# Row softmax on one core: two 30-row loads in place of four 15-row loads, and one 30-row store in place of two

## The chip, the cores and the metric

The kernel runs on one core of a Trainium2 chip. The metric is device time in microseconds (us) of one execution. Before the change it is 159.98 us, the median of three executions (159.98, 159.98 and 159.81).

## What is computed

The input is a float32 array of 16 x 1024 x 512. Each of its 16,384 rows of 512 numbers is divided by 2 and put through a softmax:

```python
x_scaled = x / 2.0
x_max = np.max(x_scaled, axis=-1, keepdims=True)
exp_x = np.exp(x_scaled - x_max)
return exp_x / np.sum(exp_x, axis=-1, keepdims=True)
```

33.55 MB are read and 33.55 MB are written.

## The kernel before

**Rows and tiles.** A row is 2,048 bytes. The 16,384 rows are spread over 128 partitions, 128 rows to each. `TILES` (lines 10 to 12) cuts these 128 into ten tiles of 3, 5 and eight times 15 rows per partition. A tile takes a block of consecutive rows of the input, and inside it each partition has `r` consecutive rows: a 15-row tile is, for each partition, one run of 30,720 bytes, both in DRAM and in the on-chip buffer. That buffer, `arena`, holds 98 rows per partition. Tiles 0 to 7 fill it. Tiles 8 and 9 go to its first 30 rows, where tiles 0, 1, 2 and a part of 3 were, so they can be loaded only when these have been stored (`LATE`, line 14).

**Compute.** ScalarE takes the exponential of x/2 in place, one row at a time, and adds the row up on the way (line 206 for the first three rows, line 275 for the others, in a loop over groups of five rows that waits at line 142 until the tile of the group has landed). VectorE takes the reciprocal of the sums (line 168) and multiplies the rows by it in place (line 171), one 15-row tile at a time, the last tile in three pieces of five rows. The maximum is not subtracted; at the end lines 182 to 198 count the rows whose sum lies in a safe interval, and if any row's does not, the whole is computed again in the plain way (lines 220 to 259). That does not happen with this input.

**Transfers and their order.** Three engines issue DMAs, each on a queue of its own:

- SyncE (SP) loads tile 0 and issues all stores in the order of the tiles (lines 213 to 216). Each store waits until the multiply of its tile is done (line 135).
- ScalarE loads tile 1 ahead of everything (line 157) and then issues the loads of tiles 2 to 7 one behind the other (lines 159 to 161), ahead of its table load and its first exponential.
- GpSimd (POOL) loads tiles 8 and 9 (lines 178 to 181). For tile 8 it waits until the exponentials of tile 6 are done (row 83, `TURN`) and until tiles 0, 1 and 2 are stored; for tile 9 until tile 3 is stored.

**The slow store.** The store of tile 1 (`SPREAD`) is cut in three by `pieces` (lines 116 to 120): four rows of all 128 partitions (8,192 bytes each), then the fifth row (2,048 bytes) of 126 partitions, then that of the last two partitions. Ahead of the store of tile 2, SP waits until all these pieces have landed:

```python
for t in range(len(tiles)):
    if t == SPREAD + 1:
        nc.sync.wait_ge(s_home[min(LATE)], landings(range(t)))
    store(nc.sync, t)
```

So the stores of tile 2 and of all later tiles are held until the last two small rows are in DRAM.

Of the kernel before, what the change touches and what calls it, by code (L numbers as in the profile page):

```python
# [10 lines left out]
    (3, 0), (5, 3), (15, 8), (15, 23), (15, 38), (15, 53), (15, 68), (15, 83), (15, 0), (15, 15),  # L11
]

LATE = {8: (0, 1, 2), 9: (3,)}
ARENA = 98

HEAD = [3]
# [2 lines left out]
SPREAD = 1  # L20
# [8 lines left out]
def kernel(  # L29
# [5 lines left out]
    nc = tc.nc  # L35
# [6 lines left out]
    xf = x.flatten_outer_dims()  # L42
    of = out.flatten_outer_dims()
    N, D = xf.shape
    P = nc.NUM_PARTITIONS
# [14 lines left out]
    tiles, base = [], 0  # L60
# [2 lines left out]
        tiles.append((base, r, at))  # L63
        base += r

    def dram(ap, t):
        b, r, _ = tiles[t]
        return ap[b * P : (b + r) * P].rearrange("(p r) d -> p r d", r=r)

    def sb(t):  # L70
        _, r, at = tiles[t]
        return arena[:, at : at + r, :]

    straight = sum(HEAD)
# [3 lines left out]
    owner = [max(t for t, (b, _, _) in enumerate(tiles) if b <= s) for s in starts]  # L78
# [9 lines left out]
            pairs.append([k])  # L88
    upto = [1 + max(j for j, ks in enumerate(pairs) if owner[ks[0]] == t) for t in range(len(tiles))]

    ld = [nc.alloc_semaphore(f"ld{t}") for t in range(len(tiles))]
    s_home = {t: nc.alloc_semaphore(f"s_home{t}") for t in LATE}
    s_near = nc.alloc_semaphore("s_near")
    s_end = nc.alloc_semaphore("s_end")
    s_exp = nc.alloc_semaphore("s_exp")
    s_go = nc.alloc_semaphore("s_go")
    s_rec = nc.alloc_semaphore("s_rec")
    s_mul = nc.alloc_semaphore("s_mul")
# [11 lines left out]
    g_rec = nc.alloc_semaphore("g_rec")  # L110
    g_mul = nc.alloc_semaphore("g_mul")

    def load(eng, t):
        eng.dma_start(out=sb(t), in_=dram(xf, t)).then_inc(ld[t], 16)  # L114

    def pieces(t):
        r = tiles[t][1]
        if t == SPREAD:
            return [(0, P, 0, r - 1), (0, 126, r - 1, r), (126, P, r - 1, r)]
        return [(0, P, 0, r)]  # L120

    stored_by = {u: s_home[t] for t, us in LATE.items() for u in us}
    for t, (_, r, at) in enumerate(tiles):
        over = {u for u, (_, ru, au) in enumerate(tiles[:t]) if at < au + ru and au < at + r}
        assert over <= {u for v, us in LATE.items() if v <= t for u in us}

    def landings(ts):
        return 16 * sum(len(pieces(t)) for t in ts)

    near = len(tiles) - 2  # L130
    sem_of = {**stored_by, near: s_near}
    at_end = landings(t for t in range(len(tiles)) if t not in sem_of)

    def store(eng, t):
        eng.wait_ge(s_mul, upto[t])
        for p, q, lo, hi in pieces(t):
            eng.dma_start(
                out=dram(of, t)[p:q, lo:hi], in_=sb(t)[p:q, lo:hi]
            ).then_inc(sem_of.get(t, s_end), 16)

    def take(eng, sem, n):
        eng.wait_ge(sem, n).then_inc(sem, -n)  # L142

    def rounds(eng, body):


        i = eng.alloc_register("general")
        eng.wait_ge(s_near, 16)
        eng.wait_ge(s_flag, 1)
        eng.reg_load(i, flag[0:1, 0:1])  # L150
        with eng.While(lambda: eng.snap(i, min_val=0, max_val=1) < 1):
            body()
            eng.reg_add(i, i, 1)

    def early():
        load(nc.sync, 0)
        load(nc.scalar, 1)

    def loads():
        for t in range(2, min(LATE)):  # L160
            load(nc.scalar, t)

    def program():

        for j, ks in enumerate(pairs):
            b, c = starts[ks[0]], sum(sizes[k] for k in ks)
            a = b % ARENA
            nc.vector.reciprocal(  # L168
                out=recip[:, b : b + c], in_=stats[:, b : b + c]
            )._wait_ge(s_exp, ks[-1] + 1).then_inc(s_rec, 1)  # L170
            nc.vector.tensor_mul(  # L171
                out=arena[:, a : a + c],
                in0=arena[:, a : a + c],
                in1=recip[:, b : b + c].unsqueeze(2).to_broadcast([P, c, D]),
            )._wait_ge(s_rec, j + 1).then_inc(s_mul, 1)

        nc.gpsimd.memset(ones[:, :], 1.0).then_inc(s_ones, 1)  # L177
        nc.gpsimd.wait_ge(s_exp, starts.index(TURN))
        for t, us in LATE.items():
            nc.gpsimd.wait_ge(s_home[t], landings(us))  # L180
            load(nc.gpsimd, t)
        nc.gpsimd.tensor_scalar(  # L182
            out=inside[:, :], in0=stats[:, :], scalar1=LO, scalar2=HI,
            op0=Alu.max, op1=Alu.min,
        )._wait_ge(s_exp, len(sizes)).then_inc(s_cnt, 1)
        nc.vector.scalar_tensor_tensor(  # L186
            out=inside[:, :], in0=inside[:, :], scalar=1.0, in1=stats[:, :],
            op0=Alu.mult, op1=Alu.is_equal, accum_out=count[:, :],
        )._wait_ge(s_cnt, 1).then_inc(s_cnt, 1)
        nc.vector.tensor_scalar(  # L190
            out=flag[:, :], in0=total[:, :], scalar1=float(N), scalar2=None, op0=Alu.is_ge,
        )._wait_ge(s_tot, 1).then_inc(s_flag, 1)


        for t in range(len(tiles)):
            nc.tensor.wait_ge(ld[t], 16).then_inc(s_go, owner.count(t))
        nc.tensor.wait_ge(s_ones, 1)
        nc.tensor.matmul(  # L198
            total[:, :], lhsT=count[:, :], rhs=ones[:, :], start=True, stop=True
        )._wait_ge(s_cnt, 2).then_inc(s_tot, 1)  # L200

        nc.scalar.preload_act_table(Exp)  # L202
        for k, c in enumerate(HEAD):
            take(nc.scalar, s_go, 1)
            for b in range(starts[k], starts[k] + c):
                ins = nc.scalar.activation(  # L206
                    out=arena[:, b], in_=arena[:, b], func=Exp, scale=0.5,
                    accum_out=stats[:, b : b + 1],
                )
            ins.then_inc(s_exp, 1)  # L210
        exponentials(straight, n_rows)

        for t in range(len(tiles)):
            if t == SPREAD + 1:
                nc.sync.wait_ge(s_home[min(LATE)], landings(range(t)))
            store(nc.sync, t)

        x_g = xf.rearrange("(t p r) d -> t p r d", p=P, r=G)  # L220
        o_g = of.rearrange("(t p r) d -> t p r d", p=P, r=G)
        data = arena[:, 0:G]

        def vector():
            for i in range(n_rows // G):
                nc.vector.reduce_max(
                    out=g_max[:, :], in_=data, axis=mybir.AxisListType.X, negate=True
                )._wait_ge(g_go, i + 1).then_inc(g_top, 1)
                nc.vector.reduce_sum(
                    out=g_sum[:, :], in_=data, axis=mybir.AxisListType.X  # L230
                )._wait_ge(g_exp, i + 1).then_inc(g_add, 1)
                nc.vector.reciprocal(
                    out=g_sum[:, :], in_=g_sum[:, :]
                )._wait_ge(g_add, i + 1).then_inc(g_rec, 1)

        def scalar():
            for i in range(n_rows // G):
                nc.scalar.activation(out=data, in_=data, func=Exp, scale=0.5)._wait_ge(
                    g_sub, i + 1
                ).then_inc(g_exp, 1)  # L240

        def gpsimd():
            nc.gpsimd.wait_ge(s_end, at_end)
            for i in range(n_rows // G):
                nc.gpsimd.dma_start(out=data, in_=x_g[i]).then_inc(g_ld, 16)
                nc.gpsimd.wait_ge(g_ld, 16 * (i + 1)).then_inc(g_go, 1)
                nc.gpsimd.tensor_add(
                    out=data, in0=data, in1=g_max[:, :].unsqueeze(2).to_broadcast([P, G, D])
                )._wait_ge(g_top, i + 1).then_inc(g_sub, 1)
                nc.gpsimd.tensor_mul(  # L250
                    out=data, in0=data, in1=g_sum[:, :].unsqueeze(2).to_broadcast([P, G, D])
                )._wait_ge(g_rec, i + 1).then_inc(g_mul, 1)
                nc.gpsimd.wait_ge(g_mul, i + 1)
                nc.gpsimd.dma_start(out=o_g[i], in_=data).then_inc(g_st, 16)
                nc.gpsimd.wait_ge(g_st, 16 * (i + 1))

        rounds(nc.vector, vector)
        rounds(nc.scalar, scalar)
        rounds(nc.gpsimd, gpsimd)
        nc.sync.wait_ge(s_near, 16)  # L260
        nc.sync.wait_ge(s_end, at_end)
# [26 lines left out]
    first = list(entry.instructions)  # L288
    at = next(k for k, i in enumerate(head) if type(i).__name__ == "InstDrain")
    entry.instructions = head[:at] + first + head[at:]  # L290
    act = []
    entry.instructions = list(entry.instructions) + [i for i in jumps if i not in act]
    nc.switch_body(here, parent=None, valid_engines=[i.engine for i in jumps])
    loads()
    program()


# [28 lines left out]
```

## Time and profile before

| what | value |
|---|---|
| median of three executions | 159.98 us |
| the profiled execution, its own time | 159.75 us |
| its span, first to last instruction | 158.4 us |
| bytes moved by DMA | 67.11 MB |
| busy ScalarE | 80.6 us (51%) |
| busy VectorE | 73.2 us (46%) |
| exponentials of a 15-row tile | 15 rows, about 0.61 us apart |
| multiply of a 15-row tile | 8.16 us |
| last multiply ends | 128.8 us |

The page has the busy shares of the engines in 40 slices of the span, and below them the busy share of the core's 16 DMA engines and what they moved. In the DMA part, q10 is ScalarE's queue, q1 is SP's and q0 is GpSimd's; a packet is what one DMA engine moves in one go, and the packets of four bytes tell a semaphore that an engine has finished its part of a transfer. A view of a stretch of time counts the packets that begin in it. The list of waits says, for each engine, what it waited for, how long in total, how many times, and the longest; SPq is SP's own sequencer, which issues stores.

### The profile page before, as it was taken

What the parts mean: (1) busy time and instruction counts of PE and PEld (TensorE: products, weight loads), DVE (VectorE), ACT (ScalarE), POOL (GpSimd) and SP (SyncE); (2) the same over time, 40 slices, a digit from 0 to 9 for tenths busy, and PEclk for the clock granted to TensorE, in tenths of its full rate; (3) what the DMA queues carried; (4) which work ended last, traced back from release to release, by engine and by line L of the source; (5) the groups of instructions that cost most, each with busy time, mean ns of one, the idle gap of its engine ahead of it and who ended that gap; (6) DMA issues with size and microseconds to landing.
All of it is one profiled execution on the core that took longest, in us unless ns stands there. A gap on an engine that the chain in (4) does not pass through costs nothing. (4 is left out here: it accounts for less than half of the span.)

```text
span 158.4 us, 658 instructions
## 1 busy us (share of the span) xinstructions
PE 0.2 (0%) x2; PEld 0.1 (0%) x2; DVE 73.2 (46%) x27; ACT 80.6 (51%) x257; POOL 2.2 (1%) x8
## 2 busy tenths in 40 slices
PE   0000000000000000000000000000000000000000
PEld 0000000000000000000000000000000000000000
DVE  0066000992994979903970029808927960000000
ACT  0780399598899980795005971991059700000000
POOL 0000000000000000001000010000000100000000
DMA  7999998999999999999898989898989898989896
GB/s 270 469 411 383 461 439 357 446 470 412 395 502 389 442 427 427 442 411 458 388 481 380 489 380 489 380 489 380 489 372 496 372 489 380 489 380 489 380 481 264
DMA packets 3024, 67.11 MB, mean 424 GB/s; under 512 B 336, under 2 KB 336, under 8 KB 720
## 3 DMA queue, kind: packets, MB, share of 16 engines
q1 hardware_dynamic: 1728, 34.34, 50.7%
q10 hardware_dynamic: 1008, 24.90, 37.0%
q0 software_dynamic: 288, 7.86, 11.5%
HBM read 33.55 MB, written 33.55 MB: 424 GB/s over the span
## 5 line engine op out<-in xcount | busy, mean ns | idle before, releaser
L275 ACT ACTIVATE arena<-arena x125 | 76.7, 615 | 40.2 <-ACTq L142 40.2
L171 DVE TENSOR_TENSOR arena<-arena,recip 128x7680 f32<-128x7680 f32 (+2 forms) x12 | 70.2, 5847 | 0.4
L168 DVE RECIPROCAL recip<-stats 128x15 f32<-128x15 f32 (+2 forms) x12 | 2.7, 224 | 55.5 <-ACT arena L275 47.3
L275 ACT ACTIVATION_READ_ACCUMULATOR arena<-arena x125 | 23.4, 187 | 0.0
L202 ACT ACT_TABLE_LOAD x1 | 1.3, 1283 | 5.0 <-issue 5.0
L114 POOL DMA_DIRECT2D arena<-in_x_dram x2 | 1.3, 631 | 90.3 <-ACT arena L275 72.3
L206 ACT ACTIVATE arena<-arena 128x512 f32<-128x512 f32 x3 | 1.9, 618 | 0.0
L182 POOL TENSOR_SCALAR inside<-stats 128x128 f32<-128x128 f32 x1 | 0.6, 631 | 32.6 <-ACT arena L275 32.6
L206 ACT ACTIVATION_READ_ACCUMULATOR arena<-arena 128x1 f32 x3 | 0.6, 185 | 0.0
L198 PE MATMUL total<-ones,count 128*1 128x1 f32 x2 | 0.2, 164 | 129.1 <-DVE inside L186 129.1
L186 DVE SCALAR_TENSOR_TENSOR inside<-inside,stats 128x128 f32<-128x128 f32 x1 | 0.3, 284 | 0.0
L190 DVE TENSOR_SCALAR flag<-total 1x1 int32<-1x1 f32 x1 | 0.1, 147 | 0.3 <-PE total L198 0.3
L198 PEld LDWEIGHTS total<-ones,count 128*1 128x1 f32 x2 | 0.1, 80 | 129.1 <-DVE inside L186 129.1
L177 POOL MEMSET ones<- 128x1 f32 x1 | 0.1, 99 | 1.1 <-POOLq L37 1.1
L310 POOL MEMSET const-float32-0.0<- 128x1 f32 x1 | 0.1, 105 | 0.2 <-issue 0.2
L310 POOL MEMSET const-bfloat16-1.0<- 128x1 bf16 x1 | 0.1, 108 | 0.0
L310 POOL MEMSET const-uint8-127<- 128x1 uint8 x1 | 0.1, 108 | 0.0
L310 POOL MEMSET const-float32-1.0<- 128x1 f32 x1 | 0.1, 105 | 0.0
L186 DVE DVE_READ_ACCUMULATOR inside<-inside,stats 128x1 f32 x1 | 0.1, 83 | 0.0
## 6 DMA issues: line engine op xcount, KB each, us to landing
out_dram<-arena SPq DMA_DIRECT2D x8, 3840.0 KB, 42.9
arena<-in_x_dram ACTq DMA_DIRECT2D x6, 3840.0 KB, 41.7
arena<-in_x_dram POOLq DMA_DIRECT2D x2, 3840.0 KB, 23.7
arena<-in_x_dram ACTq DMA_DIRECT2D x1, 1280.0 KB, 7.3
out_dram<-arena SPq DMA_DIRECT2D x1, 1024.0 KB
arena<-in_x_dram SPq DMA_DIRECT2D x1, 768.0 KB, 5.9
out_dram<-arena SPq DMA_DIRECT2D x1, 768.0 KB
out_dram<-arena SPq DMA_DIRECT2D x1, 252.0 KB
```

What stands on the lines that cost most here:

```text
L114: eng.dma_start(out=sb(t), in_=dram(xf, t)).then_inc(ld[t], 16)
L168: nc.vector.reciprocal(out=recip[:, b : b + c], in_=stats[:, b : b + c])._wait_ge(s_exp, ks[-1] + 1).then_inc(s_rec, 1)
L171: nc.vector.tensor_mul(out=arena[:, a : a + c], in0=arena[:, a : a + c], in1=recip[:, b : b + c].unsqueeze(2).to_broadcast([P, c, D]),)._w ...
L177: nc.gpsimd.memset(ones[:, :], 1.0).then_inc(s_ones, 1)
L182: nc.gpsimd.tensor_scalar(out=inside[:, :], in0=stats[:, :], scalar1=LO, scalar2=HI, op0=Alu.max, op1=Alu.min,)._wait_ge(s_exp, len(sizes) ...
L186: nc.vector.scalar_tensor_tensor(out=inside[:, :], in0=inside[:, :], scalar=1.0, in1=stats[:, :], op0=Alu.mult, op1=Alu.is_equal, accum_ou ...
L190: nc.vector.tensor_scalar(out=flag[:, :], in0=total[:, :], scalar1=float(N), scalar2=None, op0=Alu.is_ge,)._wait_ge(s_tot, 1).then_inc(s_f ...
L198: nc.tensor.matmul(total[:, :], lhsT=count[:, :], rhs=ones[:, :], start=True, stop=True)._wait_ge(s_cnt, 2).then_inc(s_tot, 1)
L202: nc.scalar.preload_act_table(Exp)
L206: ins = nc.scalar.activation(out=arena[:, b], in_=arena[:, b], func=Exp, scale=0.5, accum_out=stats[:, b : b + 1],)
L275: ins = nc.scalar.activation(out=data, in_=data, func=Exp, scale=0.5, accum_out=stats[:, r : n_rows - E + 1 + r][:, bass.ds(now, 1)],)
L310: nc = _bacc.Bacc("TRN2", target_bir_lowering=False, num_devices=1)
```

## The change

Loads and stores get lists of their own. The tiles, the arena, the exponentials and the multiplies stay as they are; what changes is which tiles share one DMA.

- Tiles 4 and 5 are loaded by one DMA, and so are tiles 6 and 7. Such a pair is one block of rows: each partition has 30 consecutive rows, a run of 61,440 bytes.
- Tiles 6 and 7 are also stored by one DMA of 30 rows, which waits for the multiplies of both. Tiles 4 and 5 are stored one at a time: each store writes half of a partition's run of 30 rows.
- Row groups of a pair may begin when the whole pair has landed, since a pair has one semaphore.
- `LATE` and the semaphores are counted by load, so tile 8 is load 6 and tile 9 load 7; what they wait for is the same.

On the queues: ScalarE issues five loads where it issued seven (10,240 bytes per partition, two of 30,720, two of 61,440), SP eleven store DMAs where it issued twelve, GpSimd two as before. The order of instructions on VectorE, GpSimd and TensorE is the same.

```diff
-LATE = {8: (0, 1, 2), 9: (3,)}
+LOADS = [(0,), (1,), (2,), (3,), (4, 5), (6, 7), (8,), (9,)]
+STORES = [(0,), (1,), (2,), (3,), (4,), (5,), (6, 7), (8,), (9,)]
+
+LATE = {6: (0, 1, 2), 7: (3,)}
...
-    def dram(ap, t):
-        b, r, _ = tiles[t]
-        return ap[b * P : (b + r) * P].rearrange("(p r) d -> p r d", r=r)
...
+    def dram(ap, ts):
+        b, r, _ = span(ts)
+        first, rows, _ = next(blocks[k] for k, us in enumerate(LOADS) if ts[0] in us)
+        assert first <= b and b + r <= first + rows
+        block = ap[first * P : (first + rows) * P].rearrange("(p r) d -> p r d", r=rows)
+        return block[:, b - first : b - first + r]
...
-    def load(eng, t):
-        eng.dma_start(out=sb(t), in_=dram(xf, t)).then_inc(ld[t], 16)
+    def load(eng, k):
+        eng.dma_start(out=sb(LOADS[k]), in_=dram(xf, LOADS[k])).then_inc(ld[k], 16)
...
-    def store(eng, t):
-        eng.wait_ge(s_mul, upto[t])
-        for p, q, lo, hi in pieces(t):
+    def store(eng, j):
+        ts = STORES[j]
+        eng.wait_ge(s_mul, upto[ts[-1]])
+        for p, q, lo, hi in pieces(j):
             eng.dma_start(
-                out=dram(of, t)[p:q, lo:hi], in_=sb(t)[p:q, lo:hi]
-            ).then_inc(sem_of.get(t, s_end), 16)
+                out=dram(of, ts)[p:q, lo:hi], in_=sb(ts)[p:q, lo:hi]
+            ).then_inc(sem_of.get(j, s_end), 16)
...
-        for t in range(len(tiles)):
-            nc.tensor.wait_ge(ld[t], 16).then_inc(s_go, owner.count(t))
+        for k, ts in enumerate(LOADS):
+            nc.tensor.wait_ge(ld[k], 16).then_inc(
+                s_go, sum(owner.count(t) for t in ts)
+            )
...
-        for t in range(len(tiles)):
-            if t == SPREAD + 1:
-                nc.sync.wait_ge(s_home[min(LATE)], landings(range(t)))
-            store(nc.sync, t)
+        for j in range(len(STORES)):
+            if j == SPREAD + 1:
+                nc.sync.wait_ge(s_home[min(LATE)], landings(range(j)))
+            store(nc.sync, j)
```

`span(ts)` gives the first row, the number of rows and the place in the arena of a group of tiles that lie behind one another.

More of the change, by code (lines that the diff above doesn't have):

```diff
@@ L64, with span, sb @@
         base += r
-    def dram(ap, t):
-        b, r, _ = tiles[t]
-        return ap[b * P : (b + r) * P].rearrange("(p r) d -> p r d", r=r)
-    def sb(t):
-        _, r, at = tiles[t]
+    def span(ts):
+        assert all(tiles[u][2] == tiles[t][2] + tiles[t][1] for t, u in zip(ts, ts[1:]))
+        return tiles[ts[0]][0], sum(tiles[t][1] for t in ts), tiles[ts[0]][2]
+    for part in (LOADS, STORES):
+        assert [t for ts in part for t in ts] == list(range(len(tiles)))
+    blocks = [span(ts) for ts in LOADS]
+    def dram(ap, ts):
[4 more added lines that the diff above has]
+        return block[:, b - first : b - first + r]
+    def sb(ts):
+        _, r, at = span(ts)
         return arena[:, at : at + r, :]
@@ L89 @@
     upto = [1 + max(j for j, ks in enumerate(pairs) if owner[ks[0]] == t) for t in range(len(tiles))]
-    ld = [nc.alloc_semaphore(f"ld{t}") for t in range(len(tiles))]
-    s_home = {t: nc.alloc_semaphore(f"s_home{t}") for t in LATE}
+    ld = [nc.alloc_semaphore(f"ld{k}") for k in range(len(blocks))]
+    s_home = {k: nc.alloc_semaphore(f"s_home{k}") for k in LATE}
     s_near = nc.alloc_semaphore("s_near")
@@ L111, with pieces, landings @@
     g_mul = nc.alloc_semaphore("g_mul")
-    def load(eng, t):
-        eng.dma_start(out=sb(t), in_=dram(xf, t)).then_inc(ld[t], 16)
-    def pieces(t):
-        r = tiles[t][1]
-        if t == SPREAD:
+    def load(eng, k):
+        eng.dma_start(out=sb(LOADS[k]), in_=dram(xf, LOADS[k])).then_inc(ld[k], 16)
+    def pieces(j):
+        r = span(STORES[j])[1]
+        if STORES[j] == (SPREAD,):
             return [(0, P, 0, r - 1), (0, 126, r - 1, r), (126, P, r - 1, r)]
         return [(0, P, 0, r)]
[L122 to L130, printed above, removed]
-    sem_of = {**stored_by, near: s_near}
-    at_end = landings(t for t in range(len(tiles)) if t not in sem_of)
-    def store(eng, t):
-        eng.wait_ge(s_mul, upto[t])
-        for p, q, lo, hi in pieces(t):
+    stored_by = {j: s_home[k] for k, js in LATE.items() for j in js}
+    for k, (_, r, at) in enumerate(blocks):
+        over = {
+            j for j, ts in enumerate(STORES)
+            if ts[0] < LOADS[k][0] and span(ts)[2] < at + r and at < span(ts)[2] + span(ts)[1]
+        }
+        assert over <= {j for v, js in LATE.items() if v <= k for j in js}
+    def landings(js):
+        return 16 * sum(len(pieces(j)) for j in js)
+    near = len(STORES) - 2
+    sem_of = {**stored_by, near: s_near}
+    at_end = landings(j for j in range(len(STORES)) if j not in sem_of)
+    def store(eng, j):
+        ts = STORES[j]
+        eng.wait_ge(s_mul, upto[ts[-1]])
+        for p, q, lo, hi in pieces(j):
             eng.dma_start(
-                out=dram(of, t)[p:q, lo:hi], in_=sb(t)[p:q, lo:hi]
-            ).then_inc(sem_of.get(t, s_end), 16)
+                out=dram(of, ts)[p:q, lo:hi], in_=sb(ts)[p:q, lo:hi]
+            ).then_inc(sem_of.get(j, s_end), 16)
     def take(eng, sem, n):
@@ L159, in loads @@
     def loads():
-        for t in range(2, min(LATE)):
-            load(nc.scalar, t)
+        for k in range(2, min(LATE)):
+            load(nc.scalar, k)
     def program():
@@ L178, in program @@
         nc.gpsimd.wait_ge(s_exp, starts.index(TURN))
-        for t, us in LATE.items():
-            nc.gpsimd.wait_ge(s_home[t], landings(us))
-            load(nc.gpsimd, t)
+        for k, js in LATE.items():
+            nc.gpsimd.wait_ge(s_home[k], landings(js))
+            load(nc.gpsimd, k)
         nc.gpsimd.tensor_scalar(
```

## The prediction

> **What bounds the kernel now.** I read the page's slices first, then the DMA part by stretches of time, then SP's list of waits and its instructions in order of time.
>
> ```profile
> DMA  7999998999999999999898989898989898989896
> GB/s 270 469 411 383 461 439 357 446 470 412 395 502 389 442 427 427 442 411 458 388 481 380 489 380 489 380 489 380 489 372 496 372 489 380 489 380 489 380 481 264
> HBM read 33.55 MB, written 33.55 MB: 424 GB/s over the span
> SPq L261 <- DMA out_dram<-arena: 29.2, 1, 29.2
> ```
>
> The DMA engines are busy in every slice, while ScalarE and VectorE are busy for about half of the span. SP's last wait, 29.2 us, is for stores alone: when the last multiply ends (128.8), three tiles' stores are still to move. The chain of waits ends there too, so compute sets nothing. By the packet records a full packet of 30,720 bytes takes 1.138 us on its engine, and 16 such streams give 432 GB/s; 67.11 MB at that rate are 155.3 us. The span holds 3 us more: the start, the end and small dips. What a change can do is to leave the DMA engines idle somewhere (each idle us is then a us at the end), or to shave these 3 us.
>
> ```profile
> q10 hardware_dynamic: 162, 4.49, 94.5%
> q1 hardware_dynamic: 141, 0.26, 6.1%
> ```
>
> This is the stretch from 37 to 48 us. Loads (q10) and the small rows of the slow store (q1) begin nearly as many packets, 162 and 141, though the ones hold seventeen times the bytes of the others. An engine gives the two queues a turn each, and a turn is one packet, whatever its size. In the packet records the semaphore packet of four bytes takes a turn as well.
>
> ```profile
> SPq L137 <- DMA out_dram<-arena: 13.0, 1, 13.0
> 49.08 0.36 SPq L137 DMA_DIRECT2D out_dram<-arena  x1
> q10 hardware_dynamic: 60, 1.66, 89.1%
> ```
>
> The first two lines, of SP's waits and of its instructions, show the hold: SP waits 13 us for tile 1's rows and issues tile 2's store at 49.08. The last small rows begin at 48.42 and 48.43 and their semaphore packets at 48.50 and 48.52, just as the load of tile 5 ends (its semaphore packets: 48.32 to 48.79). The third line is the stretch from 48.55 to 53: q1 begins no packet, and q10, with tiles 6 and 7 still to load, covers the 4 us until tile 2's store moves at 53. **This cover is what the change takes away.**
>
> **The loads, part by part.** A pair is one run of 61,440 bytes per partition, so I take one packet per partition. By the rows, packets of 2,048, 8,192 and 30,720 bytes take 0.084, 0.309 and 1.138 us: 0.0368 us per 1,000 bytes and 0.008 us each. One of 61,440 then takes 2.268 us, and a pair gives each engine 8 data packets and one semaphore packet, as one tile did. Until 27.9 us, when tile 3's load runs out, nothing changes but the start (below). From 27.9 on the records of before show the small rows taking their turns against 18 turns of loads, those of tiles 4 and 5, and ending with them. Now the 18 turns are those of both pairs. So the last small row ends with the last pair:
>
> - loads after 27.9: 16 packets x 2.268 = 36.3 us on each engine
> - small rows between them: 11.3% of the stretch from 28 to 48.55 us went to q1, 2.3 us
> - end of pair and small rows: 27.9 + 36.3 + 2.3 = 66.5 us
>
> At that moment all of tiles 0 to 7 is loaded; GpSimd's load of tile 8 cannot be issued until tile 2 is stored; and all later stores stand behind SP's wait, tiles 2 and 3 with their multiplies long done (36 and 47 us). All three queues are empty. The idle time:
>
> - from the semaphore packet to SP's issue: 49.08 - 48.52 = 0.56 us
> - from the issue to the first packet: the view does not show it for a store on idle engines. Nearest is the first load of the kernel, issued at 0.00 on idle engines:
>
> ```profile
> DMA  0000000000000000999480036779999497979994
> ```
>
> The stretch is 0 to 2.5 us in 40 slices; the first 16 are empty, 1.0 us, and by the packet records 14 of the 16 engines have begun at 1.29. I take 1.15. The other row is SP's issues under load, 10.22 and 49.08, whose packets came 3.9 us later or more; there load packets stood ahead, so it is the upper bound.
> - first packets begin slowly: the kernel's first 16 took 0.50 us in the mean where later ones took 0.234. I take 0.25, between 0 and 0.5.
>
> Together 0.56 + 1.15 + 0.25 = **1.96 us**, at the low end 1.56, with the loaded row 4.7.
>
> The Trainium skill ("DMA: Bandwidth & Descriptors", section "Latency and other measured facts") puts the first byte of such a DMA at about 0.6 us; in place of 1.15 that would be an estimate of 1.41 us of idle time. The trace's 1.0 speaks against it, though for a load.
>
> **What it saves.** 24 packets fewer per engine (16 of loads, 8 of the paired store) x 0.008 = 0.19 us. In the packet records the stretch from 52 to 54 us, where tile 2's store breaks in, moves 407 GB/s in place of 432: 0.12 us, which goes. The three DMAs fewer save no boundary: the records show tile 4's load beginning where tile 3's ended. ScalarE issues two loads fewer ahead of its table load (7 take 4.80 us), so the first exponential, at 6.25, waits for tile 0 (landed 5.90) and comes 0.2 to 0.3 us earlier, and so does the first store. At the end this gives nothing, since the DMA engines are busy anyway; it may move the small rows by one turn (first rival).
>
> **What comes later and is covered.** The first pair lands at about 48.5; tile 4 landed at 39.8 before. Exponentials of tile 4 move from 40.2 to about 49, those of tiles 5, 6 and 7 follow at 58, 68 and 77 (9.2 us a tile), multiplies 8.4 us behind each. Stores of tiles 2 and 3 run from 68 to 90, so stores 4 and 5 (multiplied by 67 and 76) are in time, and so is the store of 6 and 7 (95 us; its turn comes at about 123). Writing halves of 30-row runs changes no packet size; I cost it at nothing, and the one-sided risk of a slower DRAM pattern stays in the range. GpSimd waits for tile 2's store to land (about 79) where exponentials ended last before (73.9). Tile 8 moves from about 83 to 101 and tile 9 to 120, one turn each against stores. Its multiplies end by 133, against 128.8 before, and the last store's turn is at 150. So 17 us of cover stay, and nothing of this is on the path.
>
> **Sum.** 159.75 + 1.96 - 0.19 - 0.12 = **161.4 us**, made against the profiled execution's own 159.75 (span 158.4), which is 0.23 below the median shown.
>
> **The rivals.**
>
> 1. *The small rows finish a turn or two ahead of the last load packet* (not slower). Then SP issues at about 65, under the cover of a packet of 2.27 us, and the engines never run dry: 159.75 - 0.31 = 159.4 to 159.8. For it: the earlier start of 0.2 to 0.3 us is a quarter of a turn of 1.138, and turns at times come in twos. Against it: in before the last row came after tile 5's last packet on both engines that carry it, and both must be early. Chance 0.18.
> 2. *The run of 61,440 bytes is moved as two packets or more* (the change does not do what it says). Turns stay as they were, the hold ends at 49, and tiles 6 and 7 load beside stores 2 and 3 until 82 but land together at 84. Tile 8's load is then issued at 94 in place of 73.9, tile 9's last multiply is done at about 142, and the last store's turn is at 149: still covered, 159.7. For it: no packet in this trace is larger than 30,720. Against it: 30,720 itself is not cut, nor is any smaller run. Chance 0.10.
> 3. *A turn is several packets.* Then the small rows would be done early, with no idle time: 159.5. The records show singles, doubles at times. The Trainium skill ("DMA: Bandwidth & Descriptors", "Queues, rings and completion order") has an engine drain a packet of typically 9 to 17 descriptors before it turns to the next queue; the 162 against 141 above, with their alternation, agree with turns but not with turns that long. Chance 0.05.
> 4. *The restart on idle engines costs what it did under load* (slower still): 0.56 + 3.9 + 0.25 - 0.31 = 4.4, 164.2. It decides if the 3.9 us were the queue's own and not that of load packets ahead. The 1.0 at the start speaks against it. Chance 0.07.
>
> **How the numbers follow.** The forecast has 0.60, at 161.0 to 162.5. A measurement of this kernel tells about 0.2% (0.32 us) from no change. Faster by that: 0.07 (the low edge of rivals 1 and 3); within: 0.25 (the rest of them, and rival 2); slower: 0.68. The range must take in rivals 1 to 3, which hold a third: 159.4 to 162.6. Left out are rival 4 and the edges, some 0.12.
>
> **What would show it.** Right: SP's wait for tile 1's rows grows from 13.0 to about 31 us and ends near 67; q1 begins no packet, and no queue does, for some 1.5 to 2 us there; the slices have a dip in the 17th or 18th; the count of full load packets falls by 256, and each pair's packet takes about 2.27 us; from 69 us on the DMA engines are full to the end. Wrong: SP issues tile 2's store at 65 or earlier, with loads still moving (rival 1 or 3), or at 49 (rival 2); or the hole is 4 us (rival 4); or a second hole opens behind 100 us, which would mean that the later exponentials are not covered; or packets of 61,440 bytes are slower than 2.27 us.

## The result, and the profile after

The changed kernel takes **162.54 us** (median; 162.25 to 163.14 in six executions) against 159.86 us (159.77 to 159.98, six): a ratio of 1.017, 95% interval 1.0151 to 1.0188, slower by 2.7 us. The profiled execution took 162.25 us, its span is 160.9.

The slices of its page:

```profile
DMA  7999999797996999399999989999999959989996
GB/s 260 491 389 383 449 438 549 331 519 312 521 480 282 503 503 465 154 397 458 428 313 451 397 367 489 420 435 451 405 466 512 473 260 489 489 367 412 443 443 290
```

A slice is 4.02 us. The 17th (64.4 to 68.4 us) is the hole that was forecast: a 3 in the row of the DMA engines. Further digits below 9 in these rows can mislead, since a packet is booked where it begins; finer views follow. What SP waited for, and where that wait ends:

```profile
SPq L155 <- DMA out_dram<-arena: 31.0, 1, 31.0
SPq L281 <- DMA out_dram<-arena: 26.6, 1, 26.6
```
```profile
66.94 0.36 SPq L155 DMA_DIRECT2D out_dram<-arena  x1
```

The wait for tile 1's last rows has grown from 13.0 to 31.0 us, and tile 2's store is issued at 66.94. Why, shows in the stretch from 37 to 48 us:

```profile
q10 hardware_dynamic: 89, 4.67, 98.0%
q1 hardware_dynamic: 89, 0.35, 7.7%
```

89 packets of loads against 89 of the slow store: a turn each, as before, but a turn of the loads is now one packet of 61,440 bytes and takes 2.267 us. Then the hole itself, 64.5 to 68 us in 40 slices of 0.0875 us:

```profile
DMA  0000000000000000000010000000000000000999
q1 hardware_dynamic: 20, 0.50, 33.5%
q10 hardware_dynamic: 16, 0.00, 0.3%
```

Only beginnings count here: the last load packets began before 64.5 and run until 66.3 to 66.75. The 1 is the last small rows, at 66.3; by the packet records their semaphore packets begin at 66.38 and 66.42. Apart from the loads' own semaphore packets (the 16 of q10, the last at 66.75), the next beginning is at 67.80, and the first 16 packets of tile 2's store all begin between 67.80 and 67.94. Between loads and stores each engine is idle for 1.34 us in the mean.

**The other half.** The hole is 1.34 of the 2.5 us between the two profiled executions. The rest shows where GpSimd's load of tile 8 enters (it is issued at 78.11). From 82.5 to 84.5 us, 0.05 us a slice:

```profile
DMA  0000999900000000000000000000000000000009
q1 hardware_dynamic: 16, 0.49, 96.6%
q0 software_dynamic: 1, 0.03, 5.6%
```

All 16 engines begin a store packet within 0.2 us (82.73 to 82.87 by the records), and none begins another before 84.47. A packet of 30,720 bytes takes 1.138 us; these took 1.68 to 2.26. The same point in the kernel before, 76.8 to 78.8 us, where ScalarE's loads still run beside the stores, has two full rounds of beginnings, spread over half a microsecond:

```profile
DMA  9099999009090000000000090999900909000000
```

I summed over all packets what each took beyond its usual time, per engine. In the kernel before that is next to nothing from 60 us to the end. In the changed one it is 1.02 us from 82 to 86, 0.42 from 90 to 92.5 (where the next store enters beside the load; by then the beginnings are spread over 0.7 us again), and 0.15 elsewhere between 66 and 82. The account: 1.34 + 1.59 - 0.14 (the dip at 50 to 53 of before, gone) - 0.22 (24 packets fewer, 0.009 each) = 2.6, against 2.5 measured.

One stretch of this kind stands in every kernel here, the kernel before included, and so cancels in the account: 0.4 to 0.6 us from 12 to 16 us, where the first store enters beside the loads. In the kernel before it is 0.48 us, and the packets of that moment begin more than 1 us apart.

### The profile page after: what moved, and what is told of

The parts are those of the page before. It is cut to its first block, busy times and chain, and to the rows that moved or that the text cites. A ratio compares the mean times of both kernels' runs of the same rounds, so it can differ in the third digit from the quotient of the medians.

```text
span 160.9 us, 653 instructions
## 1 busy us (share of the span) xinstructions
PE 0.2 (0%) x2; PEld 0.1 (0%) x2; DVE 73.2 (45%) x27; ACT 80.3 (50%) x257; POOL 2.2 (1%) x8
```

## The experiments

Each kernel was timed against the kernel before on the same chip (159.82 to 159.88 us). "Stretched" is the sum above, per engine.

| kernel | us, median | ratio, 95% interval | hole | stretched where GpSimd's load and the next store enter |
|---|---|---|---|---|
| changed kernel | 162.54 | 1.0151 to 1.0188 | 1.34 | 1.44 |
| tile 1's last row whole | 160.55 | 1.0023 to 1.0051 | none | 0.56 |
| pairs as two runs | 159.88 | 0.9999 to 1.0017 | none | 0 |
| late load (row 88) | 160.56 | 1.0023 to 1.0053 | none | 0.28 |
| GpSimd stores tile 8 | 159.93 | 0.9996 to 1.0014 | none | 0 |
| pair 4, 5 only | 160.12 | 1.0004 to 1.0022 | none | 0 |
| pair 6, 7 only | 160.70 | 1.0044 to 1.0073 | none | 0.67 |
| paired loads, single stores | 162.44 | 1.0141 to 1.0167 | 1.56 | 1.34 |
| later load (row 93) | 160.53 | 1.0017 to 1.0061 | none | 0 |
| the same, with a hole | 162.93 | 1.0182 to 1.0208 | 1.61 | 1.49 |
| changed kernel, later load | 162.27 | 1.0148 to 1.0186 | 1.53 | 1.21 |
| stores stacked, no hole | 160.11 | 1.0003 to 1.0041 | none | 0.08 |
| hole, next stores held until row 98 | 162.93 | 1.0179 to 1.0229 | 1.52 | 1.44 |

The holes and the stretched time are those of the one profiled execution of each kernel.

### Is the hole all of it? Tile 1's last row in one piece

```diff
-            return [(0, P, 0, r - 1), (0, 126, r - 1, r), (126, P, r - 1, r)]
+            return [(0, P, 0, r - 1), (0, P, r - 1, r)]
```

> The change, with the last row of tile 1 stored by one DMA of 128 partitions in place of 126 and 2. That takes the slow store from 30 turns to 27 on the two engines that end it, so it should end one or two load packets (2.27 us each) ahead of the last pair, and tile 2's store should be issued at about 62 to 65 us, under cover. Theory A (all of the 2.5 us is the hole at 66.5 and what follows from it): about 159.9. Theory B (the hole is 1.34 us of it, and the rest is lost when GpSimd's load breaks into a stream of stores alone, at 82 to 92): about 161.2, with the dip still there and no hole.

```profile
SPq L155 <- DMA out_dram<-arena: 27.0, 1, 27.0
```

Three turns fewer, and the wait is 27.0 us in place of 31.0; tile 2's store is issued at 63.03, and no hole is left. **160.55 us: 2.0 of the 2.7 us are gone**, more than the hole's 1.34. Theory A is wrong by 0.7 us, theory B by as much the other way: with the hole most of the stretched packets went too (0.56 remain of 1.44). So the two seem linked, which neither theory had.

### Packet size or number of DMAs? Pairs as two runs

```diff
-        eng.dma_start(out=sb(LOADS[k]), in_=dram(xf, LOADS[k])).then_inc(ld[k], 16)
...
+        eng.dma_start(
+            out=arena[:, at : at + r, :].rearrange("p (n r) d -> p n (r d)", n=n),
+            in_=xf[b * P : (b + r) * P].rearrange("(n p r) d -> p n (r d)", n=n, p=P),
+        ).then_inc(ld[k], 16)
```

The store side takes the same layout, and tiles 6 and 7 are stored singly.

> The same pairs in one DMA each, but every tile is its own block of rows, so that a pair is two runs of 30,720 bytes per partition, and the store of tiles 6 and 7 is two DMAs again. If turns are packets (my step), the slow store ends at about 49 as before the change and there is no hole; if it was the number of DMAs that mattered, it ends near 66 and the hole stays (162.4). Tiles 6 and 7 land together at about 84, and GpSimd's load is issued at about 94, beside stores alone. Theory B then gives about 160.9 (a dip of 1.0 to 1.4 us near 98); theory A gives 159.8.

```profile
SPq L164 <- DMA out_dram<-arena: 13.9, 1, 13.9
```
```profile
50.03 0.36 SPq L164 DMA_DIRECT2D out_dram<-arena  x1
```

As few loads as in the change, but packets of 30,720 bytes: the wait is 13.9 us and ends at 50.03, there is no hole, and the time is that of before. **The turn is the packet; the number of loads and the common landing of a pair cost nothing here.** And theory B falls: the load of tile 8 enters at 94.95 beside stores alone, and no packet is stretched.

### What stretches the packets? Load time, queue and direction

Late load, on the kernel before:

```diff
-TURN = 83
+TURN = 88
```

> The kernel before, with GpSimd's load of tile 8 held until row 88 in place of row 83, so that it is issued at about 88 us, when ScalarE's loads have ended (83) and stores run alone. Nothing else changes, and the last store has about 10 us of cover. Theory B (a load that breaks into stores alone costs 1.0 to 1.4 us) gives about 160.9 to 161.3. Theory A gives 159.9, no change.

160.56: slower than before by 0.7 us, less than theory B's 1.0 to 1.4. In its profile the load enters unhindered at 90.6; 0.28 us are stretched at 96 to 100, where the next store enters. The profiled execution is the slowest of its five, 161.24.

GpSimd stores tile 8, on the kernel before:

```diff
             load(nc.gpsimd, t)
+        store(nc.gpsimd, near)
...
-            store(nc.sync, t)
+            if t != near:
+                store(nc.sync, t)
```

> The kernel before, with tile 8's store issued by GpSimd in place of SP, at about 116 to 120 us, into a stream of stores alone. If the dip at 82 to 92 comes from GpSimd's queue breaking into a single running queue, a dip of about 1 us shows near 120 and the time is about 160.9. If it comes from loads breaking into stores (the direction), there is no dip: 159.9.

159.93 and no dip: GpSimd's queue breaking into stores costs nothing by itself.

Only tiles 4 and 5 as a pair (the two lists and `LATE` changed accordingly, stores single):

```diff
-LOADS = [(0,), (1,), (2,), (3,), (4, 5), (6, 7), (8,), (9,)]
+LOADS = [(0,), (1,), (2,), (3,), (4, 5), (6,), (7,), (8,), (9,)]
```

> Only tiles 4 and 5 are loaded as a pair; everything else as before the change. The slow store's last 18 turns stand against one pair and one single tile, so it ends near 27.9 + 18.1 + 9.1 + 2.3 = 57.4 us and tile 7's load covers the restart: no hole. ScalarE's loads then end at about 71 and GpSimd's load is issued at about 77, beside stores alone. Theory A (hole only): 159.8. Theory B (load that breaks into stores alone costs 1.0 to 1.4): about 160.9 to 161.2.

```profile
SPq L155 <- DMA out_dram<-arena: 22.3, 1, 22.3
```

SP's wait ends at 58.04 (worked out: 57.4 and half a microsecond), tile 7 covers the restart, and GpSimd's load enters at 81.79 beside stores alone with nothing stretched. What is stretched, 0.42 us, lies at 60 to 62, where tile 2's store enters beside tile 7's load (0.14 at that entry in the kernel before), which fits the time: 160.12, 0.2 above before. Theory B is out for good. The issues of this kernel from 76 to 82 us are those of the changed kernel within a microsecond (GpSimd's at 77.40 against 78.11); what differs is that there the engines had run dry at 66.7.

Only tiles 6 and 7 as a pair (`STORES` and `LATE` as in the run before):

```diff
-LOADS = [(0,), (1,), (2,), (3,), (4, 5), (6, 7), (8,), (9,)]
+LOADS = [(0,), (1,), (2,), (3,), (4,), (5,), (6, 7), (8,), (9,)]
```

> Only tiles 6 and 7 are loaded as a pair; everything else as before the change. The slow store ends at 49 as before, so no hole. The pair's packets of 61,440 bytes take two thirds of the engines against stores, and the pair lands at about 76 to 78; GpSimd's load is issued at about 86, beside stores alone. Theory A: 159.8. Theory B: about 160.9 to 161.2.

160.70: within 0.2 us of theory B's range, but the wrong reason: of its 0.67 us of stretched packets 0.26 are at the load's entry, on five engines of 16. A further 0.34 us are stretched at 48 to 54, where tile 2's store enters beside the pair's load (0.14 there in the kernel before). With these the time of its profiled execution is accounted for to 0.1 us, but why the packets stretch is not.

Paired loads, single stores:

```diff
-STORES = [(0,), (1,), (2,), (3,), (4,), (5,), (6, 7), (8,), (9,)]
+STORES = [(0,), (1,), (2,), (3,), (4,), (5,), (6,), (7,), (8,), (9,)]
```

> The change with tiles 6 and 7 stored one at a time again. The paired store stands in the trace of the changed kernel from 124 to 142 us with nothing beside it, at 434 GB/s, so both theories expect no difference from the changed kernel: about 162.5 (0.06 us more for eight packets).

162.44: the paired store does nothing, the loads do all. Its trace repeats the hole (1.56) and the stretch (1.34).

### Does the hole itself stretch what comes after?

A control and the same with a hole, both on the kernel before. Control:

```diff
-TURN = 83
+TURN = 93
```

> Control for the next run: the kernel before, with GpSimd's load of tile 8 held until row 93, so that it is issued at about 89 us beside stores alone. No hole, and the engines' packets stay spread over about a microsecond. Whatever a late load costs by itself (0.4 to 0.7 us, as with row 88) shows here: 160.2 to 160.6. A theory that the entry of a load into stores alone costs 1 us in every case is already out (two runs entered so at no cost).

With a hole, also:

```diff
+            if t == 4:
+                nc.sync.wait_ge(s_home[9], 16)
             store(nc.sync, t)
```

> The same as the run before it, and tile 4's store also waits until tile 3's store has landed (at about 86 us). No load is in flight then, so the engines run dry and restart together. Theory C (the hole also puts all 16 engines in step, and in step they stall together when GpSimd's load enters and when the next store enters beside it): the control + 1.3 us for the hole + about 1 us of stretched packets in the 10 us behind it, so 162.5 to 163. Theory D (the stretched packets in the changed kernel have nothing to do with the hole): the control + 1.3, so 161.5 to 161.9, and no more stretched packets than in the control.

The control takes 160.53 (159.84 to 161.6), the kernel with a hole 162.93. Here is the entry of GpSimd's load in the control, 92.7 to 94.7 us, and then with a hole, 93.4 to 95.4:

```profile
DMA  0009909909099000000000000099099090900000
q0 software_dynamic: 16, 0.49, 57.1%
q1 hardware_dynamic: 16, 0.49, 56.9%
```
```profile
DMA  0009990000000000000000000000000000000000
q1 hardware_dynamic: 16, 0.49, 102.5%
```

In the control the 16 store packets begin over half a microsecond, and 1.14 us later come the 16 first load packets. In the other kernel the hole came at about 86 us. Here all 16 begin within 0.15 us, and for the rest of the 2 us nothing begins. The hole is 1.61 us, the stretch 0.93 at the entry and 0.56 at the next store's; the control has none there. **Theory D is out: the hole brings the stretch, as theory C said.** That being in step is what stalls the engines fits the entry of the load, but no run has them in step without a hole. At the next store's entry the beginnings are spread over 0.4 us again, and there the theory has no account of the 0.56.

The changed kernel with the load held until row 93 (the same edit of `TURN`):

> The changed kernel, with GpSimd's load of tile 8 held until row 93, so that it enters at about 90 us in place of 84. The hole stays. Theory C: the stretched packets (1.0 us at 82 to 86, 0.4 at 90 to 92) move to where the load enters now, and the time stays near 162.5. If they belong to the places 82 and 90 themselves (what is loaded and stored there), they vanish or stay behind, and the time falls to about 161.2.

162.27. The stretch moved with the load, to 87.4 (0.9 us) and 104 (0.3), and stayed: it doesn't belong to the place.

### In step, or a deep queue of stores?

Behind each hole SP had issued three stores at once. Both are on the control above.

```diff
+            if t == 4:
+                nc.sync.wait_ge(s_mul, upto[6])
             store(nc.sync, t)
```

> In every run with a hole, SP issued three stores at once behind it, so the stretched packets could come from the deep queue of stores and not from the engines being in step. Here: the load held until row 93, no hole, but the store of tile 4 waits for the multiply of tile 6 (82 us), so that the stores of tiles 4, 5 and 6 are issued at once while tile 3's is still moving (it ends at 85). Theory C (in step): as the control without the wait, no stretched packets where the load enters at about 94, 160.0 to 160.6. Theory E (a deep queue of stores): about 0.9 us of stretched packets there, 161.3 to 161.9.

```diff
+            if t == 4:
+                nc.sync.wait_ge(s_home[9], 16)
+            if t == 5:
+                nc.sync.wait_ge(s_exp, starts.index(98))
             store(nc.sync, t)
```

> The opposite: the hole at 86 us (tile 4's store waits for tile 3's landing), but tile 5's store also waits until row 98 (about 94 us), so that only one store is queued when the load enters at about 94 to 95 us. Theory C: the stretch of about 0.9 us at the entry is there, 162.3 to 163. Theory E: the stretch is gone, the hole alone stays: 161.3 to 161.9.

The entries, 92.7 to 94.7 us with the stores stacked and no hole, and 93.4 to 95.4 with a hole and tile 5's store held until row 98:

```profile
DMA  0999999009000000000000909999990090000000
q1 hardware_dynamic: 19, 0.52, 61.2%
q0 software_dynamic: 14, 0.43, 49.9%
```
```profile
DMA  0999900000000000000000000000000000000000
q1 hardware_dynamic: 16, 0.49, 104.7%
```

Stacked without a hole, two rounds begin as usual, and 0.08 us are stretched, nearly all in two packets. **A deep queue of stores alone does not stall the engines, so theory E is out.** The time is less clean than its median of 160.11: seven of the twelve executions took 159.82 to 160.16, three 161.06 to 161.19 (the profiled one among them), and two 162.3, which stand outside the interval. In the profiled one the last engine ends 1.2 us behind the next; the two longest left no trace.

With the hole all engines stall as one, at 162.93. But this run does not do what was expected of it: row 98 was done at 91.8 us, not at 94.

```profile
91.79 1.61 SPq L137 DMA_DIRECT2D out_dram<-arena  x2
```

These are the stores of tiles 5 and 6, issued 1.3 us and more ahead of the stalled packets, which begin at 93.49. So three stores were queued at the entry here too. What the run shows is that they need not be stacked at the hole: from 85.66 to 91.79 one store was queued, and the engines stayed in step. Whether a hole with a single store queued at the entry stalls them was not tested.

No run beat the kernel before.

## Why the prediction was right, and where it was short

The direction, the place and the mechanism were right; the time, 161.4, was 1.1 us short of 162.54. The measured time lies just above the forecast's own band (161.0 to 162.5) and at the upper end of the range (159.4 to 162.6), and that is in part luck: two errors partly cancel, the idle time put too high and the stretched packets put at nothing. With the idle time as measured the sum would have been 160.8.

- *One packet per partition and a turn per packet.* Right: 256 packets of 61,440 bytes are loads, each 2.267 us (worked out: 2.268), and the slow store got 89 turns against 89. The run with two runs per partition shows that packet size alone does it.
- *The last small row ends with the last pair, at 66.5 us.* Right: 66.42. SP's wait: 31 expected, 31.0 seen. Rival 1 was the weakest point and did not come; taking away three turns by hand made it come.
- *The idle time, 1.96 us.* Too high. From the semaphore packet to the issue 0.52 (0.56 taken), from the issue to the first packet 0.86 (1.15 taken, from a load at the kernel's start), and the first packets took 1.16 in place of 1.138, not 0.25 more. Idle per engine: 1.34. The Trainium skill ("DMA: Bandwidth & Descriptors", section "Latency and other measured facts") gives about 0.6 us to the first byte; counted from the issue, this trace has 0.86 for a store and 1.0 for a load, so the figure was low, but an estimate by it (1.41) would have come nearer than mine.
- *What it saves, 0.31 us.* The packets went as worked out (0.009 us each in place of 0.008). The first exponential was expected 0.2 to 0.3 us earlier; ScalarE was ready earlier, but tile 0 landed at 6.47 in place of 5.90, and it came at 6.68 in place of 6.25. It cost nothing.
- *"What comes later and is covered ... nothing of this is on the path", and "from 69 us on the DMA engines are full to the end".* **This is the step that failed.** Compute was covered as worked out (17 us of slack were never touched), and I looked for cost only there. But full engines can still be slow: behind the hole, where GpSimd's load and then the next store enter, 1.44 us go in stretched packets. Whoever counts only empty time misses it. I saw the dip of 0.12 us at 52 to 54 in the trace of before, where a store breaks into loads, and took it for a thing that goes, not for one that could grow. The larger one in the same trace, 0.48 us where the first store enters, I left out of account.
- *Rival 4* would have given 164.2 by a restart of 3.9 us. The restart was 0.86, so those 3.9 us were the load packets ahead, as argued.

What stays open: why packets stretch when another queue enters. All holes made engines begin within 0.12 to 0.15 us of each other, and all four further kernels with a hole stalled, 0.9 to 1.0 us at the load's entry. Without a hole the beginnings spread over 0.4 us and more, and at that entry six kernels had nothing stretched and one 0.08 us; but the last row whole and the pair of 6 and 7 had 0.3, on some of the engines. And where a store enters beside loads, as at 12 to 16 us, packets stretch with the beginnings far apart. So being in step goes with the long stall of all engines, and it is not needed for a shorter one. The Trainium skill ("HBM Reference", section "Latency") puts a DRAM access at 0.2 us in the mean and 2 us under high load. The 0.54 to 1.12 us that the stalled packets of the changed kernel took too long lie between the two, but no run here shows where the time is spent.

Open, too, are the 0.7 to 0.8 us that four kernels without a hole still lost (the last row whole, the late load, the later load, the pair of 6 and 7). Part of it is that the engines end apart: in the profiled executions of the first two the last engine ends 0.9 and 1.25 us behind the mean of all 16, in the kernel before 0.3, and in the kernels with a hole 0.1 to 0.3. What sets these off was not isolated.

## What to carry to other kernels

In these traces two queues share a DMA engine by turns of one packet, whatever its size (89 turns against 89, of up to 61,440 bytes against 8,192 and less). Here doubling the rows of one queue made the wait for the queue beside it grow from 13.0 to 31.0 us: a small transfer that paces something else, as tile 1's last row does, is paced by the other queue's packet size. Before merging transfers, count turns until each waiting semaphore, and look at what is still in flight when it comes.

A hole in a saturated stream can cost more than its own length: in the five kernels with one, 1.3 to 1.6 us of idle time brought another 1.2 to 1.5 us where other queues entered behind it. Look behind a hole for packets that take longer than their size asks for.

## What the runs showed of the hardware

- A run of 61,440 bytes per partition is moved as one packet: 2.267 us, 27.1 GB/s per engine. It saves 0.009 us against two of 30,720, all that longer packets bring here.
- A store on idle engines moves its first packet 0.86 us after the issue. On engines busy with packets of 30,720 bytes the same took 3.9 us.
- Of three stores issued back to back behind the hole, the third issue took 0.92 us where an issue takes 0.33 (in the changed kernel at 67.82; 0.91 in the kernel before with a hole).
- Engines in step took 1.68 to 2.26 us for a packet of 1.138 when a load's queue entered (the changed kernel); spread over 0.4 us and more, they took no more than usual in six kernels (before, two runs, the late and the later load, GpSimd's store, the pair of 4 and 5), 0.08 us more in the mean with the stores stacked, and 0.3 us more with the last row whole and the pair of 6 and 7.
- Where a store's queue enters beside loads, packets stretch without a hole: 0.4 to 0.6 us per engine at 12 to 16 us in all kernels, up to 0.42 where tile 2's store enters (the pair of 4 and 5).
